# Encoder on one core: sums and squares ordered at the begin of stages, splits of reloads ordered at the FFN's turn, and a last norm without diagonals

## The chip, the cores and the metric

The kernel runs on one core of a Trainium2 chip. The core has five engines, each with its own queue of instructions that it works off strictly in order: TensorE (PE, matrix products), VectorE (DVE), ScalarE (ACT), GpSimd (POOL) and SyncE (SP, which here only issues transfers). Engines wait for each other through semaphores. The metric is the time of one execution on the device in microseconds; less is better.

## What is computed

The reference is an encoder of two layers on 1024 tokens of width 1024. Each layer adds a mixer and a gated feed-forward network (FFN) to x, each behind an RMS norm; a last norm ends it:

```python
def rmsnorm(x, g):
    y = x * lax.rsqrt(jnp.mean(x * x, axis=-1, keepdims=True) + EPS)
    return y * g

def conv_ffn(xn, w_up, ffn_conv_w, w_down):      # D_MODEL 1024, D_FF 2048
    h = dwconv_causal(xn @ w_up, ffn_conv_w)
    g, val = h[..., :D_FF], h[..., D_FF:]
    return (jax.nn.gelu(g) * val) @ w_down

for l in range(DEPTH):                           # DEPTH 2
    h = rmsnorm(x, attn_norm_g[l])
    x = x + hybrid_mixer(h, ...)                 # conv, gated spatial and pool branches
    h = rmsnorm(x, ffn_norm_g[l])
    x = x + conv_ffn(h, w_up[l], ffn_conv_w[l], w_down[l])
return rmsnorm(x, final_norm_g)
```

## The kernel before

Activations lie as channels x tokens. The 1024 tokens are worked as two halves of 512 (x0 and x1, each eight tiles of 128 x 512), and every fp32 product is made of three fp32r matmuls: high weight by high operand, high by low, low by high. So each operand is first *split*: ScalarE rounds it to its high half (a CAST row), VectorE subtracts to get the low half (`halves`; for weights `split`, L287 and L288). A split weight stays in a ring of five buffers, a raw weight in another ring of five, and SP loads a raw weight once the low half of an older one has been made.

The wide projections (mixer in, FFN up) are blocks of seven products after Strassen. A block of two weight tiles works on operands made of x0 and x1: B11 and B21 (parts of the normed x0), T2, T3, T1, T4 and B22 (parts and differences of both). `Block.first` multiplies B11 into `run` and B21 into `c`; `second` adds the product with T2 onto `run`; `rest` computes T3 into `c`, whose copy by ScalarE is called p (L401), adds T1 onto `run`, adds T4 onto the same `c`, and B22 onto `run`. T4 writes where T3's product lay, so it can't start until ScalarE has copied p. Likewise VectorE must have made `upv` from `run` (L405) before B22's product is added there.

At the begin of each of the four stages (mixer and FFN of both layers) `start_phase` (from L502) brings in the second half: four blocks run `first`, the norm of x1 is made (eight instructions SCALAR_TENSOR_TENSOR, L485), and for each j of 0 to 3 VectorE makes a difference t (T3's operand), a second difference, and from them the sum that is T2's operand j. Then all are split. In the traces the split halves are called T_m, B_m in a mixer and T_f, B_f in an FFN; the raw x tiles are x_i or x_o.

The FFN runs 16 up blocks (`rest` with a causal convolution of three taps, gelu and a product; the result h goes to memory, its last four tiles stay as h_kept) and then turns to `down` (products pd). For the turn, eight tiles of h are loaded during block 15 (`load_h`, `early`) and split; their splits are put among block 15's steps by `pump`. Four more, h_8 to h_11, are loaded behind.

No loop in the source fixes the order within an engine. A scheduler lists all instructions and gives each engine its order; `tc.issue_after(i)` tells it to place instructions of an engine behind instruction i of that engine, as a matter of order alone.

The last norm (`finish`, for the last quarter of the result: 256 tokens) sums squares over the tiles m on VectorE, sums over channels on PE with a column of ones (st, L422), makes rs = (mean + eps)^-1/2 on GpSimd, splits rs (rp), spreads it onto two diagonals (dg, L439) and multiplies these with ones on PE to have rs as a row on all partitions (r, L452).

## Time and profile before

| | |
|---|---|
| median of 3 runs | 2721.48 us (2721.25 to 2721.61) |
| profiled run, span in the profile | 2721.56 us, 2719.7 us |
| matmuls on TensorE | 12122 |
| raw weight loads: count, size, median time to landing | 518, 256 KB, 3.4 us |
| mean granted clock of TensorE | 0.998 of full |

A row of a timeline has the start in us, the duration, the engine, the line in the kernel, the operation, output and inputs by name, shapes and how many instructions were put together; in brackets the idle time of the engine just before and what ended it. Rows of several instructions last from the first's start to the last's end; consecutive instructions of an engine overlap by some hundredths to tenths of a us, so the distance of starts is the better price. "PEld" is the weight load, which runs beside the matmul.

### The profile page before, as it was taken

How to read it: one execution, taken by the hardware profiler on the slowest of the kernel's cores; microseconds unless marked ns; L12 is line 12 of the kernel's file. 1: busy time of each engine (PE TensorE's matmuls, PEld its weight loads, DVE VectorE, ACT ScalarE, POOL GpSimd, SP SyncE). 2: the span in 40 equal slices, each digit the busy share in tenths (PEclk: the TensorE clock that was granted, in tenths of full speed). 3: DMA queues.
4: the chain of work that ended last, by engine and by line, in shares of the span. 5: the costliest groups of instructions: out<-in, count | busy, mean ns of one | idle time of the engine just before them, and what ended most of it. 6: DMA issues, size and time to landing. Idle time of an engine off the chain costs nothing.

```text
span 2719.7 us, 35012 instructions
## 1 busy us (share of the span) xinstructions
PE 2671.9 (98%) x12122; PEld 2206.4 (81%) x12122; DVE 2058.4 (76%) x2879; ACT 1254.6 (46%) x2047; POOL 370.2 (14%) x423
## 2 busy tenths in 40 slices
PE   6999999999999999999999999999999999999998
PEld 4888888888888788878888888888888888888788
DVE  7997998967756976664579988898776579666656
ACT  5645444444333554553355444444442336445434
POOL 3231112100001311100122211110000022211000
PEclk9999999999999999999999999999999999999999
DMA  9888878673357787656569778786624677774654
GB/s 241 200 221 209 214 196 215 174 267 139 122 184 201 174 204 182 164 195 204 150 154 223 202 209 225 199 208 225 217 92 142 217 177 183 194 186 112 218 180 136
DMA packets 273923, 513.72 MB, mean 189 GB/s; under 512 B 28368, under 2 KB 49616, under 8 KB 273744
## 3 DMA queue, kind: packets, MB, share of 16 engines
q1 hardware_dynamic: 219120, 411.32, 45.7%
q0 software_dynamic: 54624, 100.16, 22.4%
q8 instruction: 95, 1.56, 0.2%
q14 instruction: 84, 0.69, 0.1%
HBM read 383.44 MB, written 87.03 MB: 173 GB/s over the span
## 4 chain that ended last, share of the span: by engine, by line
PE 81%; issue 13%; DVE 3%; DMA 2%; ACT 1%; POOL 0%; SPq 0%; DVEq 0%; POOLq 0%; ACTq 0%
PE run_up L337 13%; PE pd L337 12%; PE run_gate L337 10%; PE c_up L337 9%; PE c_gate L337 7%; PE run_glu L337 5%; PE ph L337 4%; PE c_glu L337 4%; PE po L337 3%; PE run_zp L337 2%; PE run_u L337 2%; PE run_v L337 2%; PE c_u L337 2%; PE c_zp L337 2%; PE c_v L337 1%
## 5 line engine op out<-in xcount | busy, mean ns | idle before, releaser
L288 DVE TENSOR_TENSOR split<-raw,split 128x512 fp32r<-128x512 f32 (+1 forms) x570 | 376.6, 665 | 254.5 <-ACT split L287 251.3
L287 ACT CAST split<-raw 128x512 fp32r<-128x512 f32 (+1 forms) x570 | 342.8, 603 | 465.1 <-PE pd L337 146.1
L595 DVE SCALAR_TENSOR_TENSOR conv<-z_glu,par,conv 128x1011 f32<-128x1011 f32 (+7 forms) x360 | 452.5, 1264 | 7.3 <-ACT conv L593 4.5
L287 ACT CAST split<-s 128x512 fp32r<-128x512 f32 x344 | 213.5, 622 | 368.6 <-issue 127.2
L337 PE MATMUL pd<-h,split 128*128 128x512 f32 (+1 forms) x1536 | 314.7, 364 | 3.7 <-ACT split L287 1.5
L337 PEld LDWEIGHTS pd<-h,split 128*128 128x128 f32 x1536 | 262.2, 189 | 51.9 <-ACT h L359 3.5
L288 DVE TENSOR_TENSOR split<-s,split 128x512 fp32r<-128x512 f32 x344 | 235.1, 686 | 65.0 <-ACT split L287 64.6
L219 POOL DMA_DIRECT2D s<-in_wts_dram x220 | 205.9, 977 | 400.0 <-DMA s<-in_wts_dram 182.2
L219 POOL DMA_DIRECT2D s<-s x156 | 136.7, 876 | 765.3 <-DMA s<-in_wts_dram 409.4
L337 PE MATMUL run_up<-T_f,split 128*128 128x512 f32 x768 | 184.5, 389 | 2.5 <-ACT T_f L346 2.5
L337 PE MATMUL run_up<-B_f,split 128*128 128x512 f32 x768 | 183.4, 393 | 2.5 <-DVE upv L363 2.5
L337 PE MATMUL c_up<-T_f,split 128*128 128x512 f32 x768 | 183.8, 389 | 0.3 <-ACT p_up L401 0.3
L337 PE MATMUL po<-y,split 128*128 128x512 f32 x768 | 175.7, 389 | 0.0
L337 PEld LDWEIGHTS run_up<-B_f,split 128*128 128x128 f32 x768 | 144.2, 189 | 34.8 <-DVE upv L363 4.7
L337 PEld LDWEIGHTS run_up<-T_f,split 128*128 128x128 f32 x768 | 143.8, 188 | 33.4 <-ACT T_f L346 3.5
L337 PEld LDWEIGHTS c_up<-T_f,split 128*128 128x128 f32 x768 | 144.0, 188 | 31.1 <-ACT p_up L401 1.2
L337 PEld LDWEIGHTS po<-y,split 128*128 128x128 f32 x768 | 144.0, 188 | 29.8
L337 PE MATMUL c_gate<-T_m,split 128*128 128x512 f32 x576 | 138.6, 389 | 0.0
L337 PE MATMUL run_gate<-T_m,split 128*128 128x512 f32 x576 | 138.5, 389 | 0.0
L337 PE MATMUL run_gate<-B_m,split 128*128 128x512 f32 x576 | 136.3, 389 | 0.0
L337 PE MATMUL ph<-mixed,split 128*128 128x512 f32 x576 | 136.1, 394 | 0.0
L337 PE MATMUL ph<-us,split 128*128 128x512 f32 x576 | 134.2, 391 | 0.0
(265 smaller groups left out, 4375.2 us busy)
## 6 DMA issues: line engine op xcount, KB each, us to landing
raw<-in_wts_dram SPq DMA_DIRECT2D x518, 256.0 KB, 3.4
s<-in_wts_dram SPq DMA_DIRECT2D x344, 256.0 KB, 3.6
s<-in_wts_dram POOLq DMA_DIRECT2D x220, 256.0 KB, 5.2
s<-s POOLq DMA_DIRECT2D x156, 256.0 KB, 4.2
gate<-z_gate SPq DMA_DIRECT2D x48, 512.0 KB, 4.2
gt<-gate SPq DMA_DIRECT2D x96, 256.0 KB, 3.7
h<-hd SPq DMA_DIRECT2D x56, 256.0 KB, 4.9
pooled_b<-poold SPq DMA_DIRECT2D x24, 512.0 KB, 10.0
```

What stands on the lines that cost most here:

```text
L219: nc.gpsimd.dma_start(s, o, accum_op=ALU.add)
L287: nc.scalar.copy(s[:, 0, :cols], src[:, :cols])
L288: nc.vector.tensor_tensor(s[:, 1, :cols], src[:, :cols], s[:, 0, :cols].bitcast(F32), op=ALU.subtract)
L337: nc.tensor.matmul(ps[:, cols], w[:, i0, wsl], a[:, i1, cols], start=first and k == 0 and j == 0, stop=last and k == n - 1 and j == 2, ski ...
L595: nc.vector.scalar_tensor_tensor(acc[:, k:], ain[:, : S - k], col(w0 - k), acc[:, k:], op0=ALU.mult, op1=ALU.add,)
```

## The change

It has four parts.

**Start.** The squares of x1 are listed ahead of the norm of x0: the norm and split of x0 are to be issued behind the sixth square and its sum. The sums of the first norm on PE are listed before that. `start_phase` of layer 0 runs as those of the other stages (`late` false).

**Begin of stages.** In `start_phase` each of the four groups (two norm instructions, the differences, the sum and its split) is to be issued behind the sum of the group before.

**FFN's turn.** In the last up block nothing is pumped in the old places; instead four splits of h are pumped at the second and third call of `freed`, behind the subtraction that makes upv (`state["evicted"]`) and behind the last high half of a weight (`state["high"]`). The early loads of h are no longer held behind the last weight load.

**Last norm.** For the last 256 tokens the square of tile 7 isn't added on VectorE: PE sums both tiles into the same st. rs goes to PE as a column broadcast to 128 columns, as weights against the identity, one fp32 matmul of 128 x 128 for each block; rp and dg are gone there.

```diff
@@ split
+            state["high"] = nc.scalar.copy(s[:, 0, :cols], src[:, :cols]).ins
@@ Block.rest
+            state["evicted"] = add(dst22, p7, run, ALU.subtract).ins
@@ rsqrt_sums(ss, c0, nc_, n, name, diagonals=True)
+        ss = ss if isinstance(ss, list) else [ss]
+        for i, s in enumerate(ss):
+            for b in range(nb):
+                nc.tensor.matmul(st[:, b : b + 1], s[:, c0 + b * P : c0 + (b + 1) * P], ones[:, 0:1], ...)
...
+        if not diagonals:
+            return rs, nc_
@@ rsqrt_rows
+        if dg.shape[-1] == NB:
+            for b in range(nc_ // P):
+                nc.tensor.matmul(
+                    r[:, b * P : (b + 1) * P], dg[:, b : b + 1].broadcast_to([P, P]), ident,
+                    start=True, stop=True,
+                )
+            return r
@@ start_phase
+        behind = None
         for j in range(4):
+            with ExitStack() as order:
+                if behind is not None:
+                    order.enter_context(tc.issue_after(behind))
+                for k in (j, j + 4):
+                    normed_tile(x1, r, l, col, k)
+                t3.append(temp(f"t3_{name}_{j}"))
+                add(t3[j], b12, b22, ALU.subtract)
+                add(b12, b11, b12, ALU.subtract)
+                behind = add(b11, t3[j], b11, ALU.subtract).ins
+                ops["T2"].append(split_slot(f"T2_{name}_{j}", b11))
@@ ffn, rest
+            def split_early():
+                stage.append(0)
+                if len(stage) > 1:
+                    with tc.issue_after(state["evicted"]), tc.issue_after(state["high"]):
+                        pump(4)
+            ps = b.rest(
+                z2[:, half(0)], z2[:, half(1)], 0 if i == KF - 1 else 2,
+                split_early if i == KF - 1 else None,
+            )
@@ ffn
-                    early = [load_h(k, 0) for k in range(8)]
+                    early = [load_h(k, 0, False) for k in range(8)]
@@ down
+                    if cols == RIGHT and m == KD - 1:
+                        return [sq, square(None, xq, m, cols, f"n_{l}_{h}_{cols.start}")]
@@ the program
+    rows0 = rsqrt_sums(sq0, 0, H, D, "m_0_0")
+    seen = None
     for k in range(KD):
         sq1 = square(sq1, x1, k % 2 * 4 + k // 2, slice(0, H), "m_0_1")
+        if k == KD - 3:
+            seen = state["squared"], state["summed"]
+    with tc.issue_after(seen[0]), tc.issue_after(seen[1]):
+        ops = first_half(0, C_NG, x0, rows0, "m_0")
```

What this does to the engines' order is shown at three places. First VectorE at the begin of FFN layer 0. L485 is a norm instruction, L288 the low half of a weight, L347 that of an operand; t_f is the difference, z_up a result of the earlier products, and the number behind x_o_1 the group j. Before:

```order
L288 TENSOR_TENSOR split_7500<-s_0_88_7219,split_7500 128x512
L485 SCALAR_TENSOR_TENSOR x_o_1_0_6961<-x_o_1_0_6961,par_78,r_f_1_7465 128x512 x2
L485 SCALAR_TENSOR_TENSOR x_o_1_1_6963<-x_o_1_1_6963,par_78,r_f_1_7465 128x512 x2
L485 SCALAR_TENSOR_TENSOR x_o_1_2_6965<-x_o_1_2_6965,par_78,r_f_1_7465 128x512
L288 TENSOR_TENSOR split_7518<-s_0_90_7240,split_7518 128x512
L485 SCALAR_TENSOR_TENSOR x_o_1_2_6965<-x_o_1_2_6965,par_78,r_f_1_7465 128x512
L363 TENSOR_TENSOR z_up_2_7468<-c_up_2_7489,p_up_2_7487 128x512
L288 TENSOR_TENSOR split_7536<-s_0_92_7267,split_7536 128x512
L485 SCALAR_TENSOR_TENSOR x_o_1_3_6967<-x_o_1_3_6967,par_78,r_f_1_7465 128x512 x2
L363 TENSOR_TENSOR t_f_0_7554<-x_o_1_0_6961 128x512
L363 TENSOR_TENSOR t_f_1_7563<-x_o_1_1_6963 128x512
L363 TENSOR_TENSOR x_o_1_0_6961<-x_o_0_0_6634,x_o_1_0_6961 128x512
```

And now (L500 is the norm instruction, L289 and L348 the low halves):

```order
L289 TENSOR_TENSOR split_7500<-s_0_88_7219,split_7500 128x512
L500 SCALAR_TENSOR_TENSOR x_o_1_0_6961<-x_o_1_0_6961,par_78,r_f_1_7465 128x512 x2
L289 TENSOR_TENSOR split_7518<-s_0_90_7240,split_7518 128x512
L364 TENSOR_TENSOR z_up_2_7468<-c_up_2_7489,p_up_2_7487 128x512
L289 TENSOR_TENSOR split_7536<-s_0_92_7267,split_7536 128x512
L364 TENSOR_TENSOR t_f_0_7554<-x_o_1_0_6961 128x512
L364 TENSOR_TENSOR x_o_1_0_6961<-x_o_0_0_6634,x_o_1_0_6961 128x512
L289 TENSOR_TENSOR split_7600<-s_0_94_7288,split_7600 128x512
L364 TENSOR_TENSOR x_o_0_0_6634<-t_f_0_7554,x_o_0_0_6634 128x512
L500 SCALAR_TENSOR_TENSOR x_o_1_1_6963<-x_o_1_1_6963,par_78,r_f_1_7465 128x512
L364 TENSOR_TENSOR z_up_3_7516<-c_up_3_7535,p_up_3_7533 128x512
L348 TENSOR_TENSOR T_f_0_7558<-x_o_0_0_6634,T_f_0_7558 128x512
```

All eight norm instructions stood ahead of the first difference and of z_up_3 and split_7600. Now two stand ahead of split_7518, z_up_2, split_7536, the first group's differences and split_7600, and the other six behind the first group's sum, each group behind the one before.

Second ScalarE at the same begin, around the copy p_up_0 that T4 of the first block waits for. T_f_0 to T_f_3 are in turn the operands of T1 (from x_o_1) and T4 (from x_o_0), B_f those of B22. Before:

```order
L346 CAST T_f_2_7686<-x_o_1_2_6965 128x512
L346 CAST T_f_3_7689<-x_o_1_3_6967 128x512
L346 CAST T_f_0_7693<-x_o_0_0_6634 128x512
L346 CAST T_f_1_7697<-x_o_0_1_6636 128x512
L346 CAST T_f_2_7701<-x_o_0_2_6638 128x512
L287 CAST split_7722<-s_0_88_7494 128x512
L401 COPY p_up_0_7737<-c_up_0_7721 128x512
L287 CAST split_7749<-s_0_90_7619 128x512
L287 CAST split_7765<-s_0_90_7617 128x512
L287 CAST split_7781<-raw_7473 128x512
L346 CAST T_f_3_7705<-x_o_0_3_6640 128x512
L346 CAST B_f_0_7708<-x_o_1_0_6961 128x512
```

And now:

```order
L347 CAST T_f_2_7686<-x_o_1_2_6965 128x512
L347 CAST T_f_3_7689<-x_o_1_3_6967 128x512
L347 CAST T_f_0_7693<-x_o_0_0_6634 128x512
L347 CAST T_f_1_7697<-x_o_0_1_6636 128x512
L347 CAST T_f_2_7701<-x_o_0_2_6638 128x512
L347 CAST T_f_3_7705<-x_o_0_3_6640 128x512
L347 CAST B_f_0_7708<-x_o_1_0_6961 128x512
L347 CAST B_f_1_7711<-x_o_1_1_6963 128x512
L347 CAST B_f_2_7714<-x_o_1_2_6965 128x512
L347 CAST B_f_3_7717<-x_o_1_3_6967 128x512
L288 CAST split_7722<-s_0_88_7494 128x512
L402 COPY p_up_0_7737<-c_up_0_7721 128x512
```

The cast of T_f_3 and the four of B_f stood behind p_up_0, split_7749 and its followers; now all five stand ahead of split_7722 and p_up_0.

Third the turn of FFN layer 0. On VectorE split_9921 and split_9938 are low halves of down's weights, upcg and upcv (L960) the steps of the last convolution, L973 its product with the gate. Before:

```order
L360 TENSOR_TENSOR h_7_0_9772<-h_7_0_9772 128x512
L288 TENSOR_TENSOR split_9921<-raw_9841,split_9921 128x512
L288 TENSOR_TENSOR split_9938<-raw_9863,split_9938 128x512
L960 SCALAR_TENSOR_TENSOR upcg_15_9882<-z_up_15_9722,par_78,upcg_15_9882 128x1023
L960 SCALAR_TENSOR_TENSOR upcv_15_9887<-upv_15_9793,par_78,upcv_15_9887 128x1023
L960 SCALAR_TENSOR_TENSOR upcg_15_9882<-z_up_15_9722,par_78,upcg_15_9882 128x1022
L960 SCALAR_TENSOR_TENSOR upcv_15_9887<-upv_15_9793,par_78,upcv_15_9887 128x1022
L288 TENSOR_TENSOR split_9955<-raw_9924,split_9955 128x512
L973 TENSOR_TENSOR upcv_15_9887<-upcg_15_9882,upcv_15_9887 128x1024
```

And now (L982 the convolution, L1007 the product):

```order
L361 TENSOR_TENSOR h_6_0_9770<-h_6_0_9770 128x512
L361 TENSOR_TENSOR h_7_0_9772<-h_7_0_9772 128x512
L982 SCALAR_TENSOR_TENSOR upcg_15_9882<-z_up_15_9722,par_78,upcg_15_9882 128x1023
L982 SCALAR_TENSOR_TENSOR upcv_15_9887<-upv_15_9793,par_78,upcv_15_9887 128x1023
L982 SCALAR_TENSOR_TENSOR upcg_15_9882<-z_up_15_9722,par_78,upcg_15_9882 128x1022
L982 SCALAR_TENSOR_TENSOR upcv_15_9887<-upv_15_9793,par_78,upcv_15_9887 128x1022
L289 TENSOR_TENSOR split_9921<-raw_9841,split_9921 128x512
L1007 TENSOR_TENSOR upcv_15_9887<-upcg_15_9882,upcv_15_9887 128x1024
L289 TENSOR_TENSOR split_9938<-raw_9867,split_9938 128x512
L289 TENSOR_TENSOR split_9955<-raw_9924,split_9955 128x512
```

Both low halves stood ahead of the convolution's four steps. Now they stand behind them, split_9938 also behind the product. On TensorE, pd_0 and pd_1 are the first two outputs of down; before:

```order
L337 MATMUL pd_0_0_0_0_9920<-h_7_0_9772,split_9838 128x512 x3
L337 MATMUL pd_1_0_0_0_10001<-h_0_0_9758,split_9938 128x512 x3
L337 MATMUL pd_1_0_0_0_10001<-h_1_0_9760,split_9938 128x512 x3
L337 MATMUL pd_1_0_0_0_10001<-h_2_0_9762,split_9938 128x512 x3
L337 MATMUL pd_1_0_0_0_10001<-h_3_0_9764,split_9938 128x512 x3
L337 MATMUL pd_1_0_0_0_10001<-h_4_0_9766,split_9955 128x512 x3
L337 MATMUL pd_1_0_0_0_10001<-h_5_0_9768,split_9955 128x512 x3
L337 MATMUL pd_1_0_0_0_10001<-h_6_0_9770,split_9955 128x512 x3
L337 MATMUL pd_1_0_0_0_10001<-h_7_0_9772,split_9955 128x512 x3
L337 MATMUL pd_2_0_0_0_10083<-h_0_0_9758,split_10019 128x512 x2
L337 MATMUL pd_0_0_0_0_9920<-h_8_0_9896,split_9860 128x512
L337 MATMUL pd_1_0_0_0_10001<-h_8_0_9896,split_9972 128x512
```

And now:

```order
L338 MATMUL pd_0_0_0_0_9920<-h_7_0_9772,split_9838 128x512 x3
L338 MATMUL pd_1_0_0_0_10001<-h_0_0_9758,split_9938 128x512 x3
L338 MATMUL pd_1_0_0_0_10001<-h_1_0_9760,split_9938 128x512 x3
L338 MATMUL pd_1_0_0_0_10001<-h_2_0_9762,split_9938 128x512
L338 MATMUL pd_0_0_0_0_9920<-h_8_0_9896,split_9864 128x512
L338 MATMUL pd_1_0_0_0_10001<-h_2_0_9762,split_9938 128x512
L338 MATMUL pd_0_0_0_0_9920<-h_8_0_9896,split_9864 128x512 x2
L338 MATMUL pd_0_0_0_0_9920<-h_9_0_9900,split_9864 128x512 x3
L338 MATMUL pd_0_0_0_0_9920<-h_10_0_9904,split_9864 128x512
L338 MATMUL pd_1_0_0_0_10001<-h_2_0_9762,split_9938 128x512
L338 MATMUL pd_0_0_0_0_9920<-h_10_0_9904,split_9864 128x512 x2
L338 MATMUL pd_0_0_0_0_9920<-h_11_0_9908,split_9864 128x512 x3
```

After the first 24 matmuls of pd_0, the product with h_0 to h_7 of pd_1 came in one piece, and h_8 behind it. Now pd_0's products with h_8 to h_11 stand within and behind pd_1's product with h_2.

## The prediction

> **What bounds the kernel now.** I read the page first, then the list of waits on TensorE, then the timeline of each engine at the places that the change touches. The page's head:

> ```profile
> span 2719.7 us, 35012 instructions
> ...
> PE 2671.9 (98%) x12122; PEld 2206.4 (81%) x12122; DVE 2058.4 (76%) x2879; ACT 1254.6 (46%) x2047; POOL 370.2 (14%) x423
> ```

> PE is busy for 2671.9 of 2719.7 us. The change takes nothing off PE's matmuls that could be seen, so it acts only on the 47.8 us in which PE stands. The profiled run took 2721.56 us, 1.86 more than its span and 0.08 more than the median of the runs shown; I make the sum against 2721.56. The waits that the change aims at, in the list of waits (us in total, times, longest):

> ```profile
> PE run_glu L337 <- ACT T_m L346: 4.6, 3, 2.1
> ...
> PE run_up L337 <- DVE upv L363: 2.5, 2, 2.1
> PE run_up L337 <- ACT T_f L346: 2.5, 2, 1.2
> ```

> These are the begins (T_m, T_f) and the turn (upv): 9.6 us together, and with the tail's few us all that can be had. So little is to be won that what the new order makes late decides the time. Everywhere else an engine's order matters only if PE comes to wait for it.

> **The begins of stages (mixer 1 and both FFNs).** TensorE at the begin of FFN layer 0, before:

> ```profile
> 902.78 11.23 PE L337 MATMUL run_up<-T_f,split 128*128 128x512 f32 x48 [1.23 <-ACT T_f L346]
> 913.86 2.88 PE L337 MATMUL c_up<-T_f,split 128*128 128x512 f32 x12
> 916.58 2.88 PE L337 MATMUL run_up<-T_f,split 128*128 128x512 f32 x12
> 919.63 5.75 PE L337 MATMUL c_up<-T_f,split 128*128 128x512 f32 x24 [0.17 <-ACT p_up L401]
> ```

> One wait of 1.23 us, then 48 matmuls on T2 without a gap, T3, T1, and T4 at 919.63 as soon as p_up is copied. Twelve matmuls in a row start 2.72 us after one another (916.58 less 913.86), 0.227 each. VectorE there:

> ```profile
> 897.42 1.40 DVE L485 SCALAR_TENSOR_TENSOR x_o<-x_o,par,r_f 128x512 f32<-128x512 f32 x2
> 898.74 1.29 DVE L363 TENSOR_TENSOR t_f<-x_o 128x512 f32<-128x512 f32 x2
> 899.94 1.28 DVE L363 TENSOR_TENSOR x_o<-x_o,x_o 128x512 f32<-128x512 f32 x2
> ...
> 908.37 0.68 DVE L363 TENSOR_TENSOR x_o<-t_f,x_o 128x512 f32<-128x512 f32 x1
> ```

> By the starts, a norm instruction (SCALAR_TENSOR_TENSOR) takes 0.66 us and a sum or lower half 0.60. At 899.94 all eight norms are over; the fourth T2 sum starts at 908.37. ScalarE, which rounds each sum to its high half and then makes the copies:

> ```profile
> 899.36 0.63 ACT L287 CAST split<-s 128x512 fp32r<-128x512 f32 x1
> ...
> 909.09 0.62 ACT L346 CAST T_f<-x_o 128x512 fp32r<-128x512 f32 x1 [1.79 <-DVE x_o L363]
> ...
> 914.80 3.77 ACT L346 CAST T_f<-x_o 128x512 fp32r<-128x512 f32 x7
> ...
> 918.97 0.60 ACT L401 COPY p_up<-c_up 128x512 f32<-128x512 f32 x1
> ```

> Between 909.09 and 918.97 no row of ScalarE has a wait: from the cast of the fourth sum to p_up it is one chain of 9.88 us. The last eight casts in it, seven of operands and one of a weight sum, take 4.17 us (914.80 to 918.97), 0.52 each.

> The new order lets a group's norms start only behind the sum of the group before. In VectorE's new order only two norms stand ahead of the lower half of split_7518, z_up_2, split_7536 and split_7600, which follow PE. They can't be sooner than before: split_7600's cast on ScalarE ends at 900.0. Before, VectorE used that stretch for the other six norms; now it waits in it. From 900.0 to the end of the fourth sum there stand 25 instructions, six norms and 19 others: 6 x 0.66 + 19 x 0.60 = 15.4 us, so that sum ends at about 915.4 and its cast starts at 915.5, **6.4 us later** than 909.09. The first sum's cast is no sooner, since it still stands behind ScalarE's cast at 901.59, which waits for PE; so the 1.23 us stay.

> ScalarE's chain then runs on from 915.5, and it has grown. In the new order all twelve casts of T1, T4 and T3+B22 operands stand ahead of p_up, before only seven: 5 x 0.52 = 2.6 us. So p_up is copied 6.4 + 2.6 = 9.0 us later, and T4 of the first block starts at about 928.6 and not 919.63. PE meets this as gaps of some 2 us between the T2 groups and of about 3.5 us ahead of T4. No other matmuls can fill them: in PE's order B22 and the later blocks stand behind T4. Price **9.0 us** for each begin.

> The other two begins have the same form and the same end, T4 released by ScalarE's copy after 0.17 us (mixer 1, then FFN layer 1):

> ```profile
> 1411.72 1.66 PE L337 MATMUL c_glu<-T_m,split 128*128 128x512 f32 x6 [0.17 <-ACT p_glu L401]
> ...
> 2258.46 1.89 PE L337 MATMUL c_up<-T_f,split 128*128 128x512 f32 x7 [0.17 <-ACT p_up L401]
> ```

> and the same two moves in the new order. Three begins: 27.0 us. Bounds: 5.3 each if ScalarE's longer chain is hidden (the T2 products then end 12 x 0.227 behind the fourth high half, at 919.1 or a little after, not at 913.9), 10.3 if the lower halves on VectorE, 0.60 each, come behind as well.

> **The start.** Mixer 0 has the same begin, but before with another order of its own (ScalarE, then PE):

> ```profile
> 53.36 0.60 ACT L346 CAST T_m<-x_i 128x512 fp32r<-128x512 f32 x1
> ...
> 63.14 0.62 ACT L346 CAST T_m<-x_i 128x512 fp32r<-128x512 f32 x1 [1.79 <-DVE x_i L363]
> ...
> 73.02 0.60 ACT L401 COPY p_glu<-c_glu 128x512 f32<-128x512 f32 x1
> ```

> ```profile
> 61.40 0.50 PE L337 MATMUL run_glu<-T_m,split 128*128 128x512 f32 x1 [2.06 <-ACT T_m L346]
> ```

> The chain from the fourth cast to p_glu is again 9.88 us (63.14 to 73.02). Behind the first sum, which I leave at 53.3, the new order has 6 norms and 16 or 17 others ahead of the fourth: 13.6 to 14.2 us, so its cast comes at 66.9 to 67.5 instead of 63.14. I take 3.8 and the same 2.6 for the five casts: 6.4. The squares of the second half, which now stand ahead of the first half's norm, bring seven sums of 0.60 = 4.2 us to VectorE while the first operands are made. They were done later before, ahead of the second norm, which now comes that much sooner; so nearly all of the 4.2 us is given back before 53.36. I take 0.5, from 0 to 4.2. The weight loads that SP and GpSimd issue in another order there cost nothing: the later ones wait for a buffer anyway. Start: **+6.9 us**.

> **The FFN's turn.** TensorE at the turn of layer 0, with the same kind of twelve matmuls ahead of it:

> ```profile
> 1173.10 2.88 PE L337 MATMUL run_up<-T_f,split 128*128 128x512 f32 x12
> ...
> 1186.19 4.53 PE L337 MATMUL run_up<-B_f,split 128*128 128x512 f32 x12 [2.05 <-DVE upv L363]
> 1190.51 11.19 PE L337 MATMUL pd<-h,split 128*128 128x512 f32 x48
> 1202.45 0.73 PE L337 MATMUL pd<-h,split 128*128 128x512 f32 x2 [0.75 <-ACT split L287]
> 1203.66 1.66 PE L337 MATMUL pd<-h,split 128*128 128x512 f32 x6 [0.47 <-ACT h L359]
> 1206.35 0.50 PE L337 MATMUL pd<-h,split 128*128 128x512 f32 x1 [1.02 <-ACT h L359]
> 1207.07 2.33 PE L337 MATMUL pd<-h,split 128*128 128x512 f32 x9 [0.23 <-DVE h L360]
> ```

> Does upv come sooner? In the new order it stands ahead of the lower halves of h, but right behind the lower half of a weight (split_9864), whose cast on ScalarE still stands behind three casts of h that wait for DMA. It ends at 1184.7 as before, so upv stays at 1185.4 and the 2.05 us stay. I cost this part at nothing.

> What stands behind it has moved. VectorE and ScalarE:

> ```profile
> 1191.89 0.69 DVE L288 TENSOR_TENSOR split<-raw,split 128x512 fp32r<-128x512 f32 x1 [1.55 <-ACT split L287]
> ...
> 1198.33 1.22 DVE L973 TENSOR_TENSOR upcv<-upcg,upcv 128x1024 f32<-128x1024 f32 x1
> ```

> ```profile
> 1205.67 1.97 ACT L359 CAST h<-h 128x512 fp32r<-128x512 f32 x3 [2.07 <-DMA h<-hd]
> ```

> The row at 1191.89 is the lower half of down's second weight (split_9938). It now stands behind the four convolution steps and behind the product at 1198.33, so it ends at about 1200.1. PE has 24 matmuls of the first output from 1190.51, to 1196.3, and then waits 3.8 us. The loads of h_8 to h_11 come no sooner: the weight load ahead of them on SP waits for the buffer that split_9921 frees, now at 1198.4. So their casts stay at 1205.67, and PE, whose order has them ahead of the second output's h_3, waits for them too. Where the first 66 matmuls of down were issued by 1209.24 before (48, 2, 6, 1 and 9), it is now 24 + 9 + 3 + 9 = 45: 21 x 0.227 = **4.8 us**. Layer 1 has the same order, and there the first 66 lay between these two rows:

> ```profile
> 2526.25 11.04 PE L337 MATMUL pd<-h,split 128*128 128x512 f32 x48
> ...
> 2543.90 1.30 PE L337 MATMUL pd<-h_kept,split 128*128 128x512 f32 x5
> ```

> That is 17.65 us, where layer 0's 66 took 18.7 (1190.51 to 1209.24). Its last loads of h come some 0.4 us sooner, so I take 4.4 there. Both turns 9.2; bounds 0 (a product elsewhere fills it) and 12.

> **The last norm.** The steps that go lie between these rows of all engines:

> ```profile
> 2709.20 0.42 DVE L363 TENSOR_TENSOR sq_n<-sq_n,sq_n 128x256 f32<-128x256 f32 x1 [0.54 <-ACT sq_n L477]
> ...
> 2709.77 0.58 PE L422 MATMUL st_fin<-ones,sq_n 128*128 128x1 f32 x4 [1.57 <-DVE sq_n L363]
> ...
> 2711.42 0.17 DVE L433 CAST rp_fin<-rs_fin 128x2 fp32r<-128x2 f32 x1 [0.88 <-POOL rs_fin L429]
> ...
> 2712.27 0.63 PE L452 MATMUL r_fin<-dg_fin,ones_r 128*128 128x256 f32 x2 [1.92 <-DVE dg_fin L439]
> ```

> The sum to PE's first st matmul is 0.57 us (2709.20 to 2709.77); from the cast, over the diagonals, to the r matmuls 0.85 (2711.42 to 2712.27). Against that stand two more small st matmuls and r matmuls in full fp32, which the trace doesn't show in this shape: I take 0.2, by the four st matmuls' 0.58. **-1.2 us**, from -1.4 to -0.5.

> **The clock.** One row of stretches shows the only cold window after the start, 3.4 us that the list gives at half clock:

> ```profile
> 1187.40:1190.80 3.40, 3.40 (x10) 2.65 (x9) 2.94 (x5) 0.50 (x2) 0.00 (x0) 0.50 0.32 113
> ```

> It lies 1.2 us behind PE's wait of 2.05 us; its price is 4.53 less 2.88 = 1.65 us for the twelve matmuls. But 2.06 us of wait at 61.40 had no cold stretch behind it. Six new gaps of 3.5 to 3.8 us (four begins, two turns) are longer than either, and I take one cold window for each: 6 x 1.65 = **9.9 us**; bounds 0 (as at 61.40) and 19.8. [...]

> **The sum.** 27.0 + 6.9 + 9.2 - 1.2 + 9.9 = +51.8, so 2721.56 + 51.8 = 2773.4; I say **2773 us**.

> **Rivals.**

> 1. *The change does what its few words say, and the kernel is faster.* The first sums come sooner, T4 isn't later, and upv is freed from the casts of h. Then go the waits quoted first (4.6 + 2.5 + 2.5 = 9.6), the cold window (1.65) and the tail's 1.2: 12.4, to 2709. It decides at one place: whether the cast of the fourth T2 sum in FFN layer 0 starts by 909.1. Against it stand the 25 instructions behind 900.0; for it, that I read the order and not the durations under it. 6%.
> 2. *Only T2 is late.* The five casts hide behind T1, no new cold windows: 3 x 5.3 + 2.5 + 9.2 - 1.2 = 26.4, to 2748. For it, T1 and T3 give PE 5.4 us of cover; against it, ScalarE's chain has no wait in it now. 17%.
> 3. [...] 15%.
> 4. *The turn costs nothing*: split_9938 gets in ahead of the convolution because that waits on ScalarE: 2773.4 - 9.2 - 3.3, about 2761. Against it, engines here run strictly in order. 8%.
> 5. *Two cold windows for each gap*: 2783. 10%.

> The forecast has 42%, and 2% are left for no change. A difference of 0.2%, 5.4 us, is about what a measurement of this kernel can tell. The range takes in rivals 3 to 5 and nearly all of 2: 2746 to 2786. Faster 0.06, same 0.02, slower 0.92.

> **What would show it.** In the new profile at FFN layer 0's begin: the 48 T2 matmuls in four groups with waits of about 2 us on ScalarE's T_f; the fourth cast near 915.5 plus the start's delay; T4 some 9 us behind, with about 3.5 us of wait on p_up. At the turn: upv with about 2 us of wait still, and nearly 4 us after 24 matmuls of pd. In the clock: one half-speed window behind each. The forecast is wrong if the T2 groups run on without a gap, or if PE's wait ahead of T4 stays under 1 us.

## The result and the profile after

The changed kernel takes 2770.53 us (median of 4 runs, 2769.61 to 2773.88) against 2721.36 us before: slower by a factor of 1.0184 (95% interval 1.0169 to 1.0198). The prediction was 2773 us with a range of 2746 to 2786. The profiled execution is the slowest of the four, 2773.88 us with a span of 2772.1; the other three lie 3 to 4 us below it. What follows reads places in that trace, whose span is 52.4 us longer than the one before, and takes totals from the medians, +49.2 us.

The list of waits on TensorE, after:

```profile
PE run_up L338 <- ACT T_f L347: 8.9, 6, 2.2
PE run_glu L338 <- ACT T_m L347: 8.1, 6, 2.1
PE pd L338 <- DVE split L289: 7.2, 2, 3.6
PE c_up L338 <- ACT p_up L402: 6.4, 2, 3.2
PE c_glu L338 <- ACT p_glu L402: 6.4, 2, 3.2
...
PE run_up L338 <- DVE upv L364: 2.9, 2, 1.9
...
PE r_fin L461 <- POOL rs_fin L435: 1.1, 1, 1.1
```

No wait that the change aims at is gone: T2's (T_f, T_m) went from 2.5 and 4.6 us to 8.9 and 8.1, upv's from 2.5 to 2.9. Two kinds are new in size: T4's wait for p, from 0.2 us each to 3.2, and pd's for a low half, twice 3.6. Of the four parts only the last norm has shorter waits.

The begin of FFN layer 0 on TensorE, to be read beside the row of 48 matmuls and T4 at 919.63 in the prediction:

```profile
911.02 3.01 PE L338 MATMUL run_up<-T_f,split 128*128 128x512 f32 x12 [1.23 <-ACT T_f L347]
916.19 7.84 PE L338 MATMUL run_up<-T_f,split 128*128 128x512 f32 x24 [2.15 <-ACT T_f L347]
925.09 3.03 PE L338 MATMUL run_up<-T_f,split 128*128 128x512 f32 x12 [1.06 <-ACT T_f L347]
...
937.38 5.49 PE L338 MATMUL c_up<-T_f,split 128*128 128x512 f32 x12 [3.17 <-ACT p_up L402]
942.66 3.34 PE L338 MATMUL run_up<-B_f,split 128*128 128x512 f32 x12
945.84 2.88 PE L338 MATMUL c_up<-T_f,split 128*128 128x512 f32 x12
```

From T2's first matmul to T4 there were 16.85 us, now 26.36: T4 is 9.51 us later. Behind it 24 matmuls took 8.46 us (937.38 to 945.84); 24 at full clock took 5.44 in the trace of before (from 324.71). ScalarE shows both parts of those 9.5 us:

```profile
910.35 0.61 ACT L347 CAST T_f<-x_o 128x512 fp32r<-128x512 f32 x1
...
924.42 0.62 ACT L347 CAST T_f<-x_o 128x512 fp32r<-128x512 f32 x1 [3.83 <-DVE x_o L364]
...
929.98 4.27 ACT L347 CAST T_f<-x_o 128x512 fp32r<-128x512 f32 x8
934.14 2.18 ACT L347 CAST B_f<-x_o 128x512 fp32r<-128x512 f32 x4
936.22 0.62 ACT L288 CAST split<-s 128x512 fp32r<-128x512 f32 x1
936.74 0.58 ACT L402 COPY p_up<-c_up 128x512 f32<-128x512 f32 x1
```

The first cast starts 0.67 us ahead of T2's first matmul, as before. The fourth starts 13.40 us behind that matmul, before 6.31: 7.1 us late. From it to p there are 12.32 us, before 9.88: twelve casts of operands where seven stood, 2.4 us.

The turn of layer 0 on TensorE:

```profile
1206.25 4.61 PE L338 MATMUL run_up<-B_f,split 128*128 128x512 f32 x12 [1.85 <-DVE upv L364]
1210.69 6.08 PE L338 MATMUL pd<-h,split 128*128 128x512 f32 x26
1220.34 2.50 PE L338 MATMUL pd<-h,split 128*128 128x512 f32 x5 [3.57 <-DVE split L289]
1223.41 2.07 PE L338 MATMUL pd<-h,split 128*128 128x512 f32 x4 [0.57 <-ACT h L360]
1226.53 4.46 PE L338 MATMUL pd<-h,split 128*128 128x512 f32 x10 [1.05 <-ACT h L360]
1230.83 2.91 PE L338 MATMUL pd<-h_kept,split 128*128 128x512 f32 x12
```

upv still costs 1.85 us. After 24 matmuls of pd and two more that need only the high half of the next weight, PE waits 3.57 us for split_9938's low half, which VectorE makes behind the product of the last convolution, and then for h. When h_kept begins, 45 matmuls of pd are done.

The clock, in stretches behind the gaps (start and end, length, the busy time and count of PE, PEld, DVE, ACT and POOL; the last three columns are granted clock, DMA share and GB/s):

```profile
916.50:919.50 3.00, 3.00 (x8) 2.33 (x8) 2.97 (x6) 0.00 (x0) 0.96 (x2) 0.50 0.96 160
937.00:943.50 6.50, 6.12 (x14) 4.79 (x15) 4.56 (x8) 2.48 (x5) 1.34 (x2) 0.50 0.49 159
1220.50:1230.00 9.50, 7.88 (x17) 4.91 (x18) 4.33 (x7) 2.47 (x4) 0.08 (x1) 0.50 0.97 332
```

All three lie at half clock throughout, the second and third over two and three of the 3.4 us that the trace of before showed for one cold window. In all, the trace has 15 such windows between the start and the last norm, the trace of before one.

The last norm, to be read beside the four rows in the prediction:

```profile
2762.65 0.42 ACT L492 ACTIVATE sq_n<-x_d 128x256 f32<-128x256 f32 x1 [2.52 <-DVE x_d L364]
...
2763.11 0.61 PE L427 MATMUL st_fin<-ones,sq_n 128*128 128x1 f32 x4 [0.68 <-ACT sq_n L492]
...
2764.81 0.71 PE L461 MATMUL r_fin<-ident,rs_fin 128*128 128x128 f32 x4 [1.09 <-POOL rs_fin L435]
...
2765.63 2.48 DVE L1118 TENSOR_TENSOR fin<-fin,r_fin 128x512 f32<-128x512 f32 x4 [1.71 <-PE r_fin L461]
```

From the last square to the last products 2.98 us; before 4.26 (2708.75 to 2713.01).

Equal matmuls in both traces give a ledger. Each row ends where the marker starts:

| stretch, and the marker that ends it | before | after | behind so far | here | predicted |
|---|---|---|---|---|---|
| start and mixer 0: T2 of FFN 0 | 902.78 | 911.02 | 8.2 | +8.2 | +8.6 |
| begin of FFN 0: T4 of block 15 | 1181.26 | 1201.52 | 20.3 | +12.0 | +10.7 |
| turn of layer 0: T2 of mixer 1 | 1394.88 | 1421.27 | 26.4 | +6.1 | +6.5 |
| begin of mixer 1: T2 of FFN 1 | 2241.65 | 2278.76 | 37.1 | +10.7 | +10.7 |
| begin of FFN 1: T4 of block 15 | 2520.06 | 2567.99 | 47.9 | +10.8 | +10.7 |
| turn of layer 1: last x_d | 2708.23 | 2762.13 | 53.9 | +6.0 | +6.1 |
| last norm: end of the span | 2719.7 | 2772.1 | 52.4 | -1.5 | -1.2 |

(The predicted column has one cold window of 1.65 us in each of the first six.)

### The profile page after: what moved, and what is told of

It is laid out like the page before. It is cut to its first block, busy times and chain, and to the rows that moved or that the text cites. A ratio compares the mean times of both kernels' runs of the same rounds, so it can differ in the third digit from the quotient of the medians.

```text
span 2772.1 us, 34999 instructions
## 1 busy us (share of the span) xinstructions
PE 2694.5 (97%) x12128; PEld 2220.0 (80%) x12128; DVE 2063.0 (74%) x2874; ACT 1255.6 (45%) x2047; POOL 362.6 (13%) x423
## 4 chain that ended last, share of the span: by engine, by line
PE 78%; issue 12%; DVE 4%; ACT 3%; DMA 2%; POOL 0%; SPq 0%; DVEq 0%; POOLq 0%; ACTq 0%
PE pd L338 12%; PE run_up L338 11%; PE run_gate L338 9%; PE c_up L338 9%; PE c_gate L338 7%; PE run_glu L338 4%; PE ph L338 4%; PE c_glu L338 3%; PE po L338 3%; PE run_zp L338 2%; PE run_u L338 2%; PE run_v L338 2%; PE c_zp L338 2%; PE c_u L338 2%; PE c_v L338 2%
## 5 line engine op out<-in xcount | busy, mean ns | idle before, releaser
L289 DVE TENSOR_TENSOR split<-raw,split 128x512 fp32r<-128x512 f32 (+1 forms) x570 | 376.7, 665 | 273.8 <-ACT split L288 260.2
L288 ACT CAST split<-raw 128x512 fp32r<-128x512 f32 (+1 forms) x570 | 342.8, 603 | 469.6 <-PE pd L338 153.1
L288 ACT CAST split<-s 128x512 fp32r<-128x512 f32 x344 | 213.3, 621 | 384.4 <-issue 130.7
L289 DVE TENSOR_TENSOR split<-s,split 128x512 fp32r<-128x512 f32 x344 | 235.9, 687 | 85.1 <-ACT split L288 84.7
```

Of the source, the lines that this page charges most:

```text
L288: state["high"] = nc.scalar.copy(s[:, 0, :cols], src[:, :cols]).ins
L289: nc.vector.tensor_tensor(s[:, 1, :cols], src[:, :cols], s[:, 0, :cols].bitcast(F32), op=ALU.subtract)
```

## The experiments

The theory is the prediction's: VectorE's six norm instructions and ScalarE's five casts set T4 late, the two low halves behind the convolution stop the turn, and gaps bring cold windows. The rivals are told with each run. Times are medians; the kernel before, run beside them, had 2720.73, 2721.18 and 2721.15 us in the three sessions.

**One part at a time.** Four kernels, each the kernel before with one part of the change.

`e1_begin`: the order at the begins alone.

```diff
+                if behind is not None:
+                    order.enter_context(tc.issue_after(behind))
```

> Only the order at the begin of stages is put into the kernel before (all four begins; the start of the program, the turn and the last norm stay). My theory: this part alone makes most of the loss, because VectorE does six norm instructions behind PE-paced rows and ScalarE has five more casts ahead of the copy that T4 waits for. From the two traces the three later begins cost 12.0, 10.7 and 10.8 us and mixer 0 some 6 to 8: together +39 to +42 us, about 2761. T4 of the first block stands 9.5 us later behind T2's first matmul in each of the three. Rival A, the parts work on each other (the start's late squares make mixer 0's loss): under +35. Rival B, the turn makes more of the loss than the ledger by traces gives it: under +30.

Measured 2759.61 us, ratio 1.0134 (1.012 to 1.0147): +38.9 us, at the lower end of the theory's range. T4 of FFN layer 0's first block comes 26.36 us behind T2's first matmul here too:

```profile
911.68 3.01 PE L337 MATMUL run_up<-T_f,split 128*128 128x512 f32 x12 [1.23 <-ACT T_f L346]
...
938.04 4.55 PE L337 MATMUL c_up<-T_f,split 128*128 128x512 f32 x12 [3.17 <-ACT p_up L401]
```

The begins alone make four fifths of the loss, so rival B falls. Rival A's "under +35" is touched by the lower end of the interval (+32.7), but its reason fails in the trace: without the changed start, T4 in mixer 0 is already at 79.91, where it was at 73.67.

`e2_turn`: the turn alone.

```diff
+                    with tc.issue_after(state["evicted"]), tc.issue_after(state["high"]):
+                        pump(4)
+                z2[:, half(0)], z2[:, half(1)], 0 if i == KF - 1 else 2,
```

> Only the FFN's turn is changed. My theory: +12 us (6.1 in layer 0, 6.0 in layer 1), about 2733, with the wait of some 3.6 us after 26 matmuls of pd in both layers and upv's wait of about 2 us still in layer 0. Rival: with the begins as before, the loads and casts of h meet the turn in time, upv is freed and the turn gains, 2717 to 2721.

Measured 2731.55 us, ratio 1.0033 (1.0022 to 1.0043): +10.8 us. The wait of 3.63 us for a low half stands in both layers, in layer 0 as

```profile
1189.14 6.05 PE L337 MATMUL pd<-h,split 128*128 128x512 f32 x26
1198.82 1.42 PE L337 MATMUL pd<-h,split 128*128 128x512 f32 x5 [3.63 <-DVE split L288]
```

and upv's wait is 1.30 and 0.48 us. The rival falls: the turn loses without any help from the begins.

`e3_start`: the start alone (squares ahead, `late` false).

```diff
+    with tc.issue_after(seen[0]), tc.issue_after(seen[1]):
+        ops = first_half(0, C_NG, x0, rows0, "m_0")
-        start_phase(l, C_NG, x0, x1, sq1, f"m_{l}", ops, blocks, l == 0)
+        start_phase(l, C_NG, x0, x1, sq1, f"m_{l}", ops, blocks, False)
```

> Only the start is changed: squares of the second half ahead of the first norm, and mixer 0's phase run with late false; the begins keep their order. My theory: the 4.2 us of sums delay the first operands but come back before T2, so 0 to +1.5 us, 2721 to 2723. Rival: the start itself makes the 8.2 us that the trace of the whole change shows at mixer 0: 2728 to 2730. A gain, 2717 to 2720, would say that the squares were a hindrance at T2 before.

Measured 2719.07 us, ratio 0.9993 (0.9984 to 1.0002): no loss, a gain of 1.7 us that the interval doesn't secure. My theory was a little off in the sign. TensorE's second wait of 2 us on T_m in mixer 0 is gone and T4 comes at 72.33 instead of 73.67.

`e4_tail`: the last norm alone.

```diff
+        if not diagonals:
+            return rs, nc_
+                    if cols == RIGHT and m == KD - 1:
+                        return [sq, square(None, xq, m, cols, f"n_{l}_{h}_{cols.start}")]
```

> Only the last norm is changed. My theory: -1.2 to -1.5 us, about 2720, all of it between the last product and the output. Rival: the row r from fp32 matmuls is slower than the two of before, or the output's transfers end when they did: 2721 to 2722.

Measured 2719.27 us, ratio 0.9994 (0.9985 to 1.0003): -1.5 us, inside the noise by itself; the rows of the trace above carry the size.

The four add up to +46.5 us; the whole change has +49.2. The 2.7 us between are no more than the intervals of these runs leave open (e1 alone: +32.7 to +40.0). What the traces do show lies in mixer 0, where start and begin meet: in the profiles T4 stands at 73.67 before, 72.33 with the start alone, 79.91 with the begin alone and 80.57 with both, so the start's gain of 1.3 us turns into a loss of 0.7 once the new order holds.

**What in the begins costs.** Three kernels.

`e7_group0`: the order for the first group only.

```diff
-                if behind is not None:
+                if j == 1:
                     order.enter_context(tc.issue_after(behind))
```

> The kernel before with the order at the begins for the first group alone (groups 2 to 4 are free of each other). My theory: what costs is that six norm instructions stand behind rows that VectorE can do only at TensorE's pace, not the chain of the four groups. The fourth sum is as late as with the whole order, so T4 is again 9 us or more behind and the time is that of the begins alone, 2755 to 2761; T2's products run with one gap instead of three. Rival: the chain of groups is the cost; then the fourth sum comes about when it did, T4 is under 4 us late and the time is 2738 or less.

Measured 2756.35 us, ratio 1.0133 (1.0116 to 1.015): +35.2 us, nearly as slow as the whole order (+38.9, with intervals that overlap). On TensorE the groups behind the first run on almost without a gap, and T4 comes 25.46 us behind T2's first matmul, 8.6 later than before, where I had 9 or more:

```profile
907.74 3.02 PE L337 MATMUL run_up<-T_f,split 128*128 128x512 f32 x12 [1.23 <-ACT T_f L346]
913.50 7.18 PE L337 MATMUL run_up<-T_f,split 128*128 128x512 f32 x24 [2.74 <-ACT T_f L346]
...
933.20 4.61 PE L337 MATMUL c_up<-T_f,split 128*128 128x512 f32 x12 [3.19 <-ACT p_up L401]
```

The chain of the four groups isn't the cost: it adds 0.9 us to these 8.6.

`e12_freenorms`: the sums of the groups in order, the norm instructions free.

```diff
+            for k in (j, j + 4):
+                normed_tile(x1, r, l, col, k)
             with ExitStack() as order:
                 if behind is not None:
                     order.enter_context(tc.issue_after(behind))
-                for k in (j, j + 4):
-                    normed_tile(x1, r, l, col, k)
```

> The kernel before with the order at the begins for the sums alone: the eight norm instructions are free, the differences and sums of the four groups stay one group behind the other. My theory: the six norms go back into VectorE's waits; what is left of the lateness of the fourth sum is about 2.2 us (18 rows of 0.60 behind 900.0), and ScalarE's five casts stay ahead of p, 2.6 us: T4 about 4.8 us late, four times: +19 us, 2738 to 2743. Rival: the chain of groups costs what the whole order costs, 2752 or more; or without the norms nothing is lost, 2720 to 2725.

Measured 2743.3 us, ratio 1.0082 (1.0069 to 1.0096): +22.2 us, just above the theory's 2738 to 2743. In TensorE's rows T4 is 22.26 us behind T2's first matmul, 5.4 later than before where I had 4.8:

```profile
906.87 3.01 PE L337 MATMUL run_up<-T_f,split 128*128 128x512 f32 x12 [1.23 <-ACT T_f L346]
...
929.13 5.49 PE L337 MATMUL c_up<-T_f,split 128*128 128x512 f32 x12 [3.20 <-ACT p_up L401]
```

By difference, 16.7 of e1's 38.9 us come from the six norms (4.1 us of T4's place at each begin), and the rest from the sums in their order, ScalarE's casts and the clock.

`e6_b22`: the whole change, B22's split behind the copy p.

```diff
-        ops["B22"] = [split_slot(f"B22_{name}_{j}", x_part(x1, j + 4)) for j in range(4)]
+        def late():
+            with tc.issue_after(state["p"]):
+                ops["B22"] = [split_slot(f"B22_{name}_{j}", x_part(x1, j + 4)) for j in range(4)]
+        blocks[0].late = late
```

> The whole change, but the split of B22's four operands is listed behind the copy p of the stage's first block, so that four of the five added casts no longer stand ahead of it on ScalarE. My theory: ScalarE's chain sets T4, so T4 comes 4 x 0.52 = 2.1 us sooner in each of four begins: -8 us, and up to 6 more if the shorter gap (1.1 us) leaves the clock up: 2756 to 2762. Rival: VectorE's low halves hold T4 as well and ScalarE's casts are hidden: -3 at most, 2767 to 2770.

Measured 2757.38 us, 13.2 below the whole change. T4 comes 24.28 us behind T2's first matmul, 2.08 sooner than with the change, its wait is 1.10 us, and the clock stays up behind it:

```profile
906.36 3.01 PE L338 MATMUL run_up<-T_f,split 128*128 128x512 f32 x12 [1.23 <-ACT T_f L347]
...
930.64 3.50 PE L338 MATMUL c_up<-T_f,split 128*128 128x512 f32 x14 [1.10 <-ACT p_up L403]
```

```profile
930.00:940.00 10.00, 9.36 (x40) 7.41 (x41) 8.05 (x14) 6.44 (x13) 1.73 (x2) 1.00 0.61 145
```

ScalarE's chain sets T4, cast for cast (4 x 0.52 = 2.08). VectorE's low halves don't. The rest of the 13.2 us isn't parted by place: 4 x 2.08 are 8.3, and the trace has no cold window behind any of the four T4.

**The clock.** `e5_warm`: the whole change, with matmuls of no use in T4's gap; their result goes nowhere.

```diff
+                    for j in range(self.fill):        # 14 in each stage's first block
+                        state["fill"] = nc.tensor.matmul(
+                            idle, ones_r, ops["T1"][j % 4][:, 0], start=True, stop=True
+                        ).ins
```

> The whole change, with 14 matmuls of no use put between T1 and T4 of each stage's first block, where TensorE waits about 3.2 us for ScalarE's copy p (their result is read by nobody). They fill the gap: 14 x 0.227 = 3.2 us. My theory of the clock term: T4 starts as late as with the change, 26.4 us behind T2's first matmul, but the cold windows that follow T4 now (1.2 to 2.5 us in each of four begins) are gone: -4 to -7 us against the change, about 2764 to 2766. Rival A: the matmuls behind T4 are slow for want of operands, not by the clock: no change, about 2770. Rival B: the added matmuls delay T4 themselves: 2772 or more.

Measured 2763.93 us: 6.6 us below the whole change, for doing more. T4 is where it was, 26.37 us behind T2's first matmul, and what follows runs at full clock (1.00 in the row of stretches):

```profile
909.47 3.01 PE L338 MATMUL run_up<-T_f,split 128*128 128x512 f32 x12 [1.23 <-ACT T_f L347]
914.64 3.37 PE L338 MATMUL run_up<-T_f,split 128*128 128x512 f32 x12 [2.15 <-ACT T_f L347]
...
932.50 3.43 PE L415 MATMUL idle_up<-T_f,ones_r 128*128 128x512 f32 x14
935.84 3.02 PE L338 MATMUL c_up<-T_f,split 128*128 128x512 f32 x12
938.70 2.88 PE L338 MATMUL run_up<-B_f,split 128*128 128x512 f32 x12
```

```profile
935.00:942.00 7.00, 7.00 (x31) 5.51 (x31) 5.72 (x10) 3.36 (x7) 1.18 (x2) 1.00 0.44 126
```

With the change 24 matmuls behind T4 took 8.46 us, here 5.57 (935.84 to 941.41). Over the four begins the two traces have 29.75 and 22.26 us for them: 7.5 us for five cold windows. Both rivals fall: the slow matmuls behind T4 were the clock's. The 6.6 us are not the price of these windows alone, since this trace also lacks two cold windows in T2 and the one behind upv, which the filling doesn't touch.

**The turn.** `e9_turnlow`: the turn alone, two of down's weights listed ahead of the last convolution.

```diff
+            if i == KF - 1:
+                split_to(state["used"] + AHEAD + 2)
             g = conv3(z1, 2 * i, f"upcg_{tag}_{i}")
```

> The turn alone as changed, with two of down's weights listed for their split ahead of the last convolution, so that their low halves stand ahead of its four steps again. My theory: the 3.6 us of wait in the second output and what follows are gone, and upv is where it was: 2719 to 2723. Rival: the loads of h and their order on TensorE make the loss: 2727 to 2732.

Measured 2720.69 us, ratio 1.0 (0.999 to 1.0009): the turn's loss is gone. In layer 0 the wait after 26 matmuls of pd is gone; what is left is 0.35 us after 38 of them, for the low half of the next weight, and upv's 1.72:

```profile
1189.44 8.78 PE L337 MATMUL pd<-h,split 128*128 128x512 f32 x38
1198.57 2.59 PE L337 MATMUL pd<-h,split 128*128 128x512 f32 x10 [0.35 <-DVE split L288]
```

On VectorE the two low halves stand at 1191.85, ahead of the convolution at 1193.06; in e2 they stood at 1196.35 and 1198.08. To within the interval their place was the whole cost.

`e10_upv`: this, with upv put ahead. The splits of h and of down's weights are held behind upv on VectorE.

```diff
-                    with tc.issue_after(state["evicted"]), tc.issue_after(state["high"]):
+                    with tc.issue_after(state["evicted"]):
...
+                if self.upv_first:                    # in block 15, at T4's and B22's operands
+                    order.enter_context(tc.issue_after(state["evicted"]))
```

> The turn mended: the splits of h and of down's weights stand behind upv on VectorE, so that upv waits for no load of h, and the low halves of down's weights stand ahead of the last convolution. My theory: TensorE no longer waits for upv (0.2 to 2.05 us in layer 0, 0.4 to 1.1 in layer 1, and a cold window where there was one); part of it comes back as longer waits for the loads h_8 to h_11: -1 to -4 us, 2717 to 2720. Rival: those loads set the end of the turn and take all of it back: 2720.5 to 2722.

Measured 2718.53 us, ratio 0.9992 (0.9983 to 1.0): -2.6 us, in the middle of the theory's range, with an interval that just touches no change. TensorE's rows show the wait for upv gone:

```profile
1180.18 2.88 PE L337 MATMUL c_up<-T_f,split 128*128 128x512 f32 x12
1182.90 2.88 PE L337 MATMUL run_up<-B_f,split 128*128 128x512 f32 x12
1185.62 8.78 PE L337 MATMUL pd<-h,split 128*128 128x512 f32 x38
1195.16 2.56 PE L337 MATMUL pd<-h,split 128*128 128x512 f32 x10 [0.77 <-DVE split L288]
```

`e11_best`: the mended turn, the changed start and the changed last norm, the begins as before.

> The mended turn with the changed start and the changed last norm, and the begins as before: the parts that the runs so far show as harmless or better. My theory: the gains add, -1.7 (start), -1.5 (last norm) and -1 to -4 (turn): 2714 to 2717. Rival: they don't add, or are noise: 2719 to 2722.

Measured 2714.07 us, ratio 0.9975 (0.9964 to 0.9985): 7.1 us faster than the kernel before, and 56 faster than the changed one. The single gains make 2.6 + 1.7 + 1.5 = 5.8; none of the three is clear of no change by its own interval, the 7.1 us are (4.1 at the least).

## Why the prediction was right

**The begins.** The step held: VectorE waits at PE-paced rows with the norms behind them, the fourth sum is late, ScalarE's chain carries that to p and adds five casts. Sizes: the fourth cast 7.1 us late and not 6.4, the chain 2.4 us longer and not 2.6, T4 9.5 us and not 9.0. The 0.7 us missing in the first are in VectorE's rows: 25 instructions at 0.66 and 0.60 left out a wait of 0.20 for the first high half, and the second difference, which three times takes 0.72 us (914.07 to 914.79) where it took 0.60. e12 and e6 moved the norms and the casts apart and got each one's price.

**The start** was put at +6.4 for the new order and +0.5 for the squares. T4 in mixer 0 came 6.9 us later (73.67 to 80.57). The order alone makes 6.2 of them (e1, 79.91). The squares alone don't cost: e3 shows a small gain, inside its interval.

**The turn.** The step held: upv not sooner (predicted 2.05 us, measured 1.85), a wait of 3.8 us (3.57) for split_9938's low half, 45 matmuls instead of 66. e9 puts the low halves back and the loss is gone.

**The last norm**: -1.2 predicted, -1.5 in the ledger.

**The clock** was the step with the least ground, and its form was off though its sum was near. I took one cold window for each of six gaps. Behind these six the trace has ten (one, two, one and one behind the four T4, three and two behind pd's waits), four more in T2 and one behind upv, which the kernel before had too. Those in T2 cost little: in e5 FFN 0 has none there, and T4 is at 26.37 us all the same. The five behind T4 cost 7.5 us in the traces, 1.4 to 1.7 each, so the second window behind T4 is what sets FFN 0 (+12.0) off from the two begins after it (+10.7 and +10.8). In the two turns, cold windows and the waits for h lie on one another and weren't parted by a run; that their +6.1 and +6.0 us fit is no evidence for one window each.

**The rivals.** Rival 1 (faster, 2709) failed at its own point: the cast of the fourth sum came 7.1 us late. Rival 2 (casts hidden) fell with e6; its 2.5 us for the start is worked out from no row. Rival 3 (the clock stays up: the forecast without its 9.9 us, about 2763) fell with e5, rival 4 at pd's 3.57 us. Rival 5 was nearer in the number of cold windows (ten of its twelve), but its sum is 12 us above the measured time. That the time came within 3 us of the sum has some luck in it: the runs of the changed kernel themselves lie 4 us apart, and a gap of 3.17 us ahead of T4 was followed by one cold window in mixer 0 and by two in FFN 0, which nothing in the trace of before told.

## What to carry to other kernels

An order edge that brings one result forward also moves everything behind it past whatever the engine must wait for there: count what the engine did in those waits before, here six norm instructions at each begin, since that work now comes after them, on the path. A copy that frees a PSUM tile (p here) is as much on the path as the operand that one looks at, and casts that slip ahead of it cost one for one (four of them 2.08 us in e6). Where two stages share an engine, list the next stage's first operands before the last stage's tail work; it was worth 10.9 us here (e2 to e9), and moving upv ahead of reloads perhaps 2.6 more, which the interval doesn't secure.

## What the runs showed of the hardware

| trace | step of the grid | TensorE stands in it | granted clock in the next step |
|---|---|---|---|
| before, gap ahead of 61.40 | 57.59 to 61.00 | 1.66 us | 1.00 |
| before, upv | 1183.99 to 1187.40 | 2.05 us | 0.50 |
| changed, T2 of FFN 0 | 912.85 to 916.26 | 2.16 us | 0.50 |
| e5_warm, T2 of FFN 0 | 910.33 to 913.75 | 1.26 us | 1.00 |
| e5_warm, T2 of FFN 0 | 913.75 to 917.16 | 0.96 us | 1.00 |

In that part of these two traces, twelve steps at full clock in which TensorE stood for 1.67 us or more were each followed by one at half clock; in every other step at full clock it stood for 1.66 us at most, and full clock followed. The two nearest, 1.66 us (before, 57.59) and 1.67 us (changed, 1424.84), are nearly alike and went different ways, so no limit is shown by them. Of the changed kernel's steps at half clock, those with 0.64, 0.86, 1.05 and 0.90 us (from 936.74, 1220.04, 1223.46 and 2585.38) were followed by another, and those with 0.58 us (from 79.99) or less by full clock. In FFN 0, whose T4 has two cold windows behind it, T4 started 0.64 us into the first; in mixer 0, which has one, 0.58 us. In e6 the gap of 1.10 us ahead of FFN 0's T4 was followed by full clock (1.00 from 930 to 940).

Filling the gap ahead of T4 with matmuls of no use took 7.5 us off the rows behind T4, and the kernel was faster by 6.6 us.
